# Moving the splits and sums behind the scan from GpSimd to VectorE in a one-core hybrid SSD / gated-MLP block

## The chip, the core and the metric

The kernel runs on one core of a Trainium2 chip, as one launch. The metric is the device time of one execution in microseconds. Five engines work side by side, each with a queue that it takes in order: TensorE (PE in the profile) for matmuls, ScalarE (ACT) for activations and copies, VectorE (DVE) and GpSimd (POOL) for elementwise work, SyncE (SP) for issuing DMAs. Matmul results land in PSUM; everything else is in SBUF or HBM.

## The reference, cut to what matters

```python
h   = rmsnorm(x, norm1_w) * (1 + sc1) + sh1          # sc1, sh1, g1, ... from c @ w_ada
proj = h @ w_in                                       # z, xbc, dt, sc_b, sc_c, sc_h
y_ssd = group_rmsnorm(ssd_scan(silu(conv(xbc)), dt) * silu(z))      # chunked scan
y_sc  = group_rmsnorm(sc_b * causal_dwconv(sc_c * sc_h, sc_conv_w)) # short convolution
x   = x + g1 * (concat(y_ssd, y_sc) @ w_out)          # out projection
h   = rmsnorm(x, norm2_w) * (1 + sc2) + sh2
u   = causal_dwconv(h @ w_up, ffn_conv_w) + ffn_conv_b # up projection, 2 x 2816 columns
x   = x + g2 * ((silu(u_gate) * u_value) @ w_down)    # down projection
out = rmsnorm(x)                                      # all float32, 1024 x 1024
```

## The kernel before, in words

**Number format.** Every large product is float32 made from three matmuls. `split` (lines 113 to 121) writes a rounded copy `hi` of a half page (128 x 512) with ScalarE (line 116) and the rest `lo = src - hi` with a second engine (line 117), VectorE unless `eng` names GpSimd; `mm3` (lines 123 to 127) then multiplies hi by hi, hi by lo and lo by hi. A matmul on an operand thus waits for one ScalarE and one VectorE or GpSimd instruction.

**Seven products instead of eight.** The short convolution, the out projection, the up and the down projection use a two-by-two scheme with seven block products (weights A11, A12, S1 to S4, A22; moving operands B11, B21, T1 to T4, B22). The weight sums S1 to S4 are made on the chip from the loaded halves: for a pair of weight pages `prep` (lines 539 to 571) issues two loads of 512 KB (lines 544, 545), four elementwise sums on the engine `sums` (line 558 for S3, line 561 for S2, S1 and S4, in place) and seven splits. The list that `prep` returns is emitted piecemeal between the products of the pair before (`take`).

**Stages, in order of time in the profiled execution.** Norm and first projection; the scan with the z projection (to about 380 us), in which GpSimd also sums weights for later (`combine`) and does two steps of the scan; the short convolution as 12 pairs (`prep_s(p)`, `pair_s`), whose sums are on VectorE for p = 0 to 3 and on GpSimd for p = 4 to 11; beside it `mod_half` (line 835) forms c @ w_ada on VectorE from loads of 256 KB; the out projection (about 600 to 776 us), where `product` calls `operand` for each step, which splits one half page of activations and one of weights, the weight's split on GpSimd in `m1` and `m2`; in `m2` GpSimd also subtracts two halves of y. Then the second norm (`x_norm`: ScalarE squares, eleven small VectorE instructions on 128 x 1, lines 97 to 106, a ScalarE scale), transposes, `half0` and `f1_tiles`, which make the moving operands B and T (`put` splits them; B22 and T4 and the difference behind T4 are on GpSimd); the up projection as 22 pairs (`prep_u(p)`), whose sums are on GpSimd except for p = 1; the down projection, which uses no GpSimd.

**What sets the order.** The engines' queues are not in the order of the text: a planner simulates the engines and emits, for each engine, the ready instruction that stands earliest; `tc.high_priority(offset=n)` lets instructions stand n places earlier. Which engine an instruction is on therefore also changes the order of the others on that engine. Buffers come from rings of fixed size: `raw` has 3 pages (4 in the up projection), `t3`, which holds the sum for S3, has one.

Of the kernel before, what the change touches and what calls it, by code (L numbers as in the profile page):

```python
# [36 lines left out]
def block_kernel(ctx: ExitStack, tc: tile.TileContext, x, crow, w_adat, w_m, w_z, w_dt,  # L37
                 w_out, w_up, w_down, vecs, rows, fnw, consts, out):
    nc = tc.nc
# [14 lines left out]
    def nm(s):  # L54
        uid[0] += 1
        return f"{s}{uid[0]}"

    def big():
        return pg.tile([P, T], F32, tag="pg", name=nm("pg"))

    def bank():
        return ps.tile([P, 512], F32, tag="ps", name=nm("ps"))
# [13 lines left out]
    def halves(page):  # L76
        return page[:, 0:512], page[:, 512:]
# [35 lines left out]
    def split(hi, lo, src, scale=None, eng=None):  # L113

        if scale is None:
            nc.scalar.activation(hi, src, AF.Copy)  # L116
            (eng or nc.vector).tensor_tensor(lo, src, hi.bitcast(F32), op=ALU.subtract)  # L117
        else:
            nc.scalar.activation(hi, src, AF.Copy, scale=scale)
            nc.vector.scalar_tensor_tensor(lo, src, scale, hi.bitcast(F32), op0=ALU.mult,  # L120
                                           op1=ALU.subtract)
# [125 lines left out]
    for k in range(ND):  # L247
# [3 lines left out]
        for q in range(2):  # L251
            s = slice(q * 512, q * 512 + 512)
            o = bank()
# [42 lines left out]
    o = bank()  # L296
# [34 lines left out]
    o = bank()  # L331
# [7 lines left out]
    o = bank()  # L339
# [46 lines left out]
    def sub(o, i0, i1, eng=None):  # L386
        (eng or nc.vector).tensor_tensor(o, i0, i1, op=ALU.subtract)  # L387
# [130 lines left out]
    wts = {}  # L518
# [20 lines left out]
    def prep(p, srcs, s3_tile, two, sums, early=None):  # L539

        rg, rv = wraw(), wraw()
        have = p in wts
        W = wts.setdefault(p, {})
        nc.sync.dma_start(rg, srcs[0])
        nc.sync.dma_start(rv, srcs[1])
        a11, a12 = halves(rg)
        a21, a22 = halves(rv)
        s3 = []

        def sp(name, src, eng=early):  # L550
            def f():
                W[name] = w_half()
                split(W[name][0], W[name][1], src if src is not None else s3[0], eng=eng)
            return f

        def sub3():
            s3.append(s3_tile())
            sums.tensor_tensor(s3[0], a11, a21, op=ALU.subtract)  # L558

        def tt(o, i0, i1, op):  # L560
            return lambda: sums.tensor_tensor(o, i0, i1, op=op)  # L561

        first = [] if have else [sp("A11", a11, None)] + ([sp("A12", a12, None)] if two else [])
        rest = [sub3, tt(a21, a21, a22, ALU.add), tt(a11, a21, a11, ALU.subtract),
                sp("S2", a11), sp("S1", a21), sp("S3", None)]
        if not two and not have:
            rest.append(sp("A12", a12))
        rest += [tt(a12, a12, a11, ALU.subtract), sp("S4", a12), sp("A22", a22)]
        if p == ("s", 0):
            rest.insert(7, rest.pop(5))  # L570
        return first + rest
# [6 lines left out]
    def prep_s(p):  # L578
        return prep(("s", p), [w_m[i] for i in spairs[p]],
                    lambda: psc[0].tile([P, 512], F32, tag="t3", bufs=1, name=nm("s3")), p < 2,  # L580
                    nc.gpsimd if p > 3 else nc.vector)

    psc = [None]

# [187 lines left out]
    with tc.high_priority(offset=100):  # L772
        for f in w0:
            f()
        gs, vl = big(), bank()
# [68 lines left out]
    for p in range(1, NS):  # L844
# [3 lines left out]
        gs, vl = (big(), nxt_vl) if p > 1 else (gs1, vl1)  # L848
# [114 lines left out]
    def acc_banks():  # L963
        return [bank() for c in range(4)]

    def big_banks():
        return [*halves(big()), *halves(big())]
# [11 lines left out]
    def dmm(o, c, op, start, stop, more=False):  # L979
        ah, al, bh, bl = op  # L980
        cs = slice(c * P, (c + 1) * P)
        mm3(o, ah[:, cs], al[:, cs], bh, bl, start, stop, more)
# [7 lines left out]
    def product(f, n, ring, o=None, i0=0, i1=None, pops=1, eng=None, more=False):  # L990

        o = o or acc_banks()
        for i in range(i0, n if i1 is None else i1):
            op = operand(f, i, ring, eng)
            for c in range(4):
                dmm(o[c], c, op, i == 0 and not more, i == n - 1, more)
            defer(pops)
        return o
# [13 lines left out]
    NM2 = 4  # L1012
# [18 lines left out]
    def load_o(i, page, half):  # L1031
        fetch()
        return ahead.pop(0)
# [4 lines left out]
    m1, _, _, _, m3, m7, m4 = sw_operands(Yo, load_o)  # L1038

    def m2(i):  # L1040
        gl, gr, vl, vr = Yo(i)
        return vl, load_o(i, 0, 1), [lambda: sub(gl, gl, gr, nc.gpsimd)]

    def m6(i):
        gl, gr, vl, vr = Yo(i)
# [54 lines left out]
    later += [lambda: ssd_load(1, (0, 1)), lambda: ssd_load(1, (2, 3)), last_pair]  # L1100
    later += [lambda: ssd_load(1, (4, 5)), lambda: ssd_load(1, (6, 7))]
    pgs = hhalf(F32)
    o = product(m1, 8, ring_o, i1=7, pops=2, eng=nc.gpsimd)
    later += [lambda i=i: sc_pair(i, 1) for i in range(3)]
    o2 = product(m2, 8, ring_o, big_banks(), i1=NM2, eng=nc.gpsimd)
    op = operand(m1, 7, ring_o)
    for c in range(4):
        dmm(o[c], c, op, False, True)
# [5 lines left out]
    for c in range(4):  # L1114
        nc.scalar.activation(acc[c], o[c], AF.Copy)
    oa = o
    o = product(m2, 8, ring_o, o2, NM2, eng=nc.gpsimd)
    c11 = hset()
    for c in range(4):
        add(c11[c], o[c], acc[c])  # L1120
# [50 lines left out]
    f0, f1 = [None] * ND, [None] * ND  # L1171

    def half0(k):
        f0[k] = f_tile(0, k)
        o = OPS["B11" if k < 4 else "B21"]
        o[k % 4] = hpage()
        split(o[k % 4][0], o[k % 4][1], f0[k], eng=nc.gpsimd if k % 2 else nc.vector)

    for c in range(4):
        later += [lambda c=c: gate(c12[c], c, 1), lambda c=c: x_norm(c)]  # L1180
# [17 lines left out]
    def prep_u(p):  # L1198
        def s3_tile():
            if p == 0:  # L1200
                return s3_first
            return pv[0].tile([P, 512], F32, tag="t3", bufs=1, name=nm("s3"))
        return prep(p, [w_up[2 * p], w_up[2 * p + 1]], s3_tile, p < 1,
                    nc.vector if p == 1 else nc.gpsimd, nc.gpsimd if p == 0 else None)

    w0 = prep_u(0)
    s3_first = yhalf()
# [4 lines left out]
    wts[1] = {}  # L1212
    for n, f in zip(("A11", "A12"), halves(t)):
        wts[1][n] = w_half()
        split(*wts[1][n], f, eng=nc.gpsimd)
    for f in w0[2:5]:
        f()
    w0 = w0[5:]
# [14 lines left out]
    def put(name, k, src, eng=None):  # L1233
        n = nput[0]
        nput[0] += 1
        if n < 8:
            d = hpage()
        elif n < 12:
            d = halves(tpage(F32R))
        elif n == 15:  # L1240
            d = small(F32R), small(F32R)
        else:
            d = yhalf(F32R), yhalf(F32R)
        OPS[name][k] = d
        split(d[0], d[1], src, eng=eng)
# [23 lines left out]
    w1 = prep_u(1)  # L1269
# [20 lines left out]
            put("T3", k, f1[k])  # L1290
        prod(V[0][0], "S3", "T3", 0, True, ks=[k])
    for k in range(4):
        put("B22", k, f1[k + 4], nc.gpsimd)
    for k in range(4):
        sub(f0[k + 4], f0[k + 4], f0[k], nc.gpsimd)
        put("T4", k, f0[k + 4], nc.gpsimd)
    hd = [pd.tile([P, T], F32, name=f"hd{p}") for p in range(NF - 1)]


# [66 lines left out]
    for p in range(NF):  # L1366
        nxt = w1 if p == 0 else prep_u(p + 1) if p + 1 < NF else sum(map(early_operand, range(3)), [])
        vl = V[p][0]
        if p > 1:
            G[p] = big()  # L1370
        gl, gr = halves(G[p])
# [34 lines left out]
    o = acc_banks()  # L1406
# [46 lines left out]
    m1, m2, m5, m6, m3, m7, m4 = sw_operands(Yd, load_d)  # L1453
# [17 lines left out]
    o = product(m1, NQ, ring, o, NE)  # L1471
# [4 lines left out]
    o = product(m2, NQ, ring)  # L1476
# [62 lines left out]
    o = product(m5, NQ, ring)  # L1539
# [3 lines left out]
    o = product(m6, NQ, ring)  # L1543
# [4 lines left out]
    o = product(m3, NQ, ring)  # L1548
# [4 lines left out]
    o = product(m7, NQ, ring)  # L1553
# [6 lines left out]
    o = product(m4, NQ, ring, [big()[:, 0:512], bank(), bank(), big()[:, 0:512]], i1=NQ - NL)  # L1560
# [87 lines left out]
```

## Time and profile before

| quantity | before |
|---|---|
| median of 3 runs | 1467.11 us (1466.14 to 1467.79) |
| profiled execution, its own time | 1469.52 us |
| span in that execution, first to last instruction | 1467.7 us |
| TensorE busy | 1388.9 us (95%), 6159 matmuls |
| VectorE busy | 1176.8 us (80%), 1882 instructions |
| ScalarE busy | 731.3 us (50%) |
| GpSimd busy | 309.3 us (21%), 213 instructions |
| mean granted TensorE clock | 0.979 of full speed |

Busy shares are means over stages with different limits, so the profile is read by stretches of the span. All times of rows are microseconds from the span's start unless marked ns. A matmul of 512 columns shows as some 0.39 us, but matmuls overlap, so TensorE is judged by its idle time and by the number of matmuls in a stretch. The granted clock stands at 1.00 (2.4 GHz) or 0.50 (1.2 GHz); a mean between them tells the share of the two in the stretch. Waiting instructions show as idle time in front of them, with the instruction that ended it.

### The profile page before, as it was taken

What the parts mean: (1) busy time and instruction counts of PE and PEld (TensorE: products, weight loads), DVE (VectorE), ACT (ScalarE), POOL (GpSimd) and SP (SyncE); (2) the same over time, 40 slices, a digit from 0 to 9 for tenths busy, and PEclk for the clock granted to TensorE, in tenths of its full rate; (3) what the DMA queues carried; (4) which work ended last, traced back from release to release, by engine and by line L of the source; (5) the groups of instructions that cost most, each with busy time, mean ns of one, the idle gap of its engine ahead of it and who ended that gap; (6) DMA issues with size and microseconds to landing.
All of it is one profiled execution on the core that took longest, in us unless ns stands there. A gap on an engine that the chain in (4) does not pass through costs nothing.

```text
span 1467.7 us, 17850 instructions
## 1 busy us (share of the span) xinstructions
PE 1388.9 (95%) x6159; PEld 1113.9 (76%) x6159; DVE 1176.8 (80%) x1882; ACT 731.3 (50%) x1272; POOL 309.3 (21%) x213
## 2 busy tenths in 40 slices
PE   4999999999999999998998699999999999999997
PEld 2788876777777777876886477888888888888885
DVE  7988868978898785599489799777777776889688
ACT  6633365666544434344486453444444444545463
POOL 0000032322012322261014733332333330000000
PEclk9999999999999999999999799999999999999999
DMA  8878964336454431785335132222222222856322
GB/s 319 299 267 316 310 199 164 136 103 222 152 173 154 140 122 61 253 253 184 114 116 172 58 129 101 86 86 82 77 87 86 87 86 101 316 207 209 100 101 101
DMA packets 89723, 232.18 MB, mean 158 GB/s; under 512 B 10296, under 2 KB 11016, under 8 KB 89632
## 3 DMA queue, kind: packets, MB, share of 16 engines
q1 hardware_dynamic: 89584, 231.00, 45.9%
q8 instruction: 48, 0.79, 0.2%
q14 instruction: 43, 0.35, 0.1%
q10 hardware_dynamic: 48, 0.05, 0.0%
HBM read 178.93 MB, written 52.08 MB: 157 GB/s over the span
## 4 chain that ended last, share of the span: by engine, by line
PE 63%; DVE 19%; DMA 6%; issue 5%; ACT 4%; POOL 1%; SPq 0%; DVEq 0%; POOLq 0%; ACTq 0%
PE ps L125 11%; PE ps L126 11%; PE ps L127 11%; PE pg L125 8%; PE pg L126 8%; PE pg L127 8%; DVE wl L117 3%; PE ps L485 2%; DVE sm L835 1%; DMA sm<-in_w_adat 1%; DMA cmb<-in_w_down 1%; ACT wh L116 1%; DVE cmb L387 1%; DVE T L373 1%; PE ps L493 1%
## 5 line engine op out<-in xcount | busy, mean ns | idle before, releaser
L116 ACT ACTIVATE wh<-raw 128x512 fp32r<-128x512 f32 (+1 forms) x272 | 173.0, 656 | 263.6 <-POOL raw L561 142.9
L117 DVE TENSOR_TENSOR wl<-raw,wh 128x512 fp32r<-128x512 f32 (+1 forms) x252 | 212.3, 855 | 78.7 <-ACT wh L116 72.6
L125 PE MATMUL pg<-H,wh 128*128 128x512 f32 x464 | 185.8, 402 | 10.5 <-ACT wh L116 6.2
L127 PE MATMUL pg<-H,wl 128*128 128x512 f32 x464 | 184.0, 397 | 1.7 <-DVE wl L117 1.7
L126 PE MATMUL pg<-H,wh 128*128 128x512 f32 x464 | 184.8, 398 | 0.4 <-DVE H L117 0.4
L125 PEld LDWEIGHTS pg<-H,wh 128*128 128x128 f32 x464 | 88.8, 192 | 32.1 <-ACT wh L116 7.3
L125 PE MATMUL ps<-H,wh 128*128 128x512 f32 x272 | 109.1, 402 | 3.8 <-ACT u L1265 3.8
L558 POOL TENSOR_TENSOR s<-raw,raw 128x512 f32<-128x512 f32 x28 | 53.5, 1912 | 278.4 <-DVE wl L117 166.6
L126 PE MATMUL ps<-H,wh 128*128 128x512 f32 x272 | 109.1, 401 | 3.2 <-DVE H L117 3.2
L127 PE MATMUL ps<-H,wl 128*128 128x512 f32 x272 | 108.0, 397 | 1.5 <-DVE wl L117 1.5
L126 PE MATMUL ps<-rg,rg 128*128 128x512 f32 x274 | 106.8, 390 | 0.0
L127 PE MATMUL ps<-rg,rg 128*128 128x512 f32 x274 | 106.6, 390 | 0.0
L127 PEld LDWEIGHTS pg<-H,wl 128*128 128x128 f32 x464 | 88.7, 191 | 21.5 <-DVE wl L117 3.2
L125 PE MATMUL ps<-rg 128*128 128x512 f32 x274 | 104.8, 390 | 0.0
L126 PEld LDWEIGHTS pg<-H,wh 128*128 128x128 f32 x464 | 88.7, 191 | 20.8 <-DVE H L117 2.5
L561 POOL TENSOR_TENSOR raw<-raw 128x512 f32<-128x512 f32 x58 | 85.9, 1492 | 78.6 <-DVE wl L117 69.1
L116 ACT ACTIVATE rg<-hp 128x512 fp32r<-128x512 f32 x85 | 51.6, 626 | 66.3 <-PE ps L127 46.1
L117 DVE TENSOR_TENSOR rg<-hp,rg 128x512 fp32r<-128x512 f32 x85 | 56.9, 684 | 18.2 <-ACT rg L116 18.0
L1330 DVE SCALAR_TENSOR_TENSOR cv<-ps,vec,cv 128x511 f32<-128x511 f32 (+2 forms) x132 | 67.8, 564 | 1.5 <-ACT cv L1326 1.4
L1309 DVE SCALAR_TENSOR_TENSOR cv<-pg,vec,cv 128x1023 f32<-128x1023 f32 (+1 forms) x44 | 56.2, 1277 | 15.4 <-ACT cv L1304 15.4
L662 DVE TENSOR_TENSOR pg<-pg,u 128x512 f32<-128x512 f32 x68 | 47.2, 694 | 25.3 <-PE pg L127 24.9
L487 POOL TENSOR_TENSOR xq<-xq,rw 128x512 f32<-128x512 f32 x16 | 19.0, 1186 | 221.3 <-issue 134.2
(379 smaller groups left out, 3513.5 us busy)
## 6 DMA issues: line engine op xcount, KB each, us to landing
raw<-in_w_up SPq DMA_DIRECT2D x45, 512.0 KB
raw<-in_w_m SPq DMA_DIRECT2D x36, 512.0 KB
sm<-in_w_adat SPq DMA_DIRECT2D x48, 256.0 KB
hd<-cv SPq DMA_DIRECT2D x21, 512.0 KB
hp<-hd SPq DMA_DIRECT2D x21, 512.0 KB
wr<-tdn SPq DMA_DIRECT2D x33, 256.0 KB
bc<-in_w_adat SPq DMA_DIRECT2D x16, 512.0 KB
seg<-ccd SPq DMA_DIRECT2D x16, 512.0 KB
```

The costliest lines, as they stand in the source:

```text
L116: nc.scalar.activation(hi, src, AF.Copy)
L117: (eng or nc.vector).tensor_tensor(lo, src, hi.bitcast(F32), op=ALU.subtract)
L125: nc.tensor.matmul(o, ah, bh, start=start, stop=False, skip_group_check=more)
L126: nc.tensor.matmul(o, ah, bl, start=False, stop=False, skip_group_check=more)
L127: nc.tensor.matmul(o, al, bh, start=False, stop=stop, skip_group_check=more)
L485: nc.tensor.matmul(y[:, h * HD:(h + 1) * HD], seg[:, h, :], xd[:, h * HD:(h + 1) * HD], start=True, stop=True)
L487: nc.gpsimd.tensor_tensor(hv(xg), hv(xg), rw[:, 2, g * 8:g * 8 + 8].unsqueeze(2).to_broadcast([P, 8, HD]), op=ALU.mult)
L558: sums.tensor_tensor(s3[0], a11, a21, op=ALU.subtract)
L561: return lambda: sums.tensor_tensor(o, i0, i1, op=op)
L662: nc.vector.tensor_tensor(o, i0, i1, op=ALU.add)
L1309: nc.vector.scalar_tensor_tensor(t[:, i:], g[:, :T - i], col(V_FW + (2 - i) * 44 + j), t[:, i:], op0=ALU.mult, op1=ALU.add)
L1330: nc.vector.scalar_tensor_tensor(o, v, col(V_FW + (2 - i) * 44 + j), o, op0=ALU.mult, op1=ALU.add)
```

## The change

All elementwise work that stood on GpSimd from the short convolution to the end of the up projection is given to VectorE: the four sums of `prep_s` for p = 4 to 11 (32 instructions), those of `prep_u` for p = 0 and p = 2 to 21 (84), the weight splits of `m1` and `m2` (15), the subtraction in `m2` (8), the odd splits of `half0` (4), the early splits of pair 0 and pair 1 of the up projection (7), the splits for B22 and T4 (8) and the subtraction for T4 (4): 162 instructions of 128 x 512 each. One piece of order changes as well: the first five entries of pair 1's list (three sums, the splits of S2 and S1) are emitted between the B22 splits and the T4 subtractions instead of later, in the loop. GpSimd keeps its work in the first projection and the scan. No DMA, matmul or ScalarE instruction is added or removed.

```diff
     def prep_s(p):
@@ in the call of prep
-                    nc.gpsimd if p > 3 else nc.vector)
+                    nc.vector)
     def m2(i):
         gl, gr, vl, vr = Yo(i)
-        return vl, load_o(i, 0, 1), [lambda: sub(gl, gl, gr, nc.gpsimd)]
+        return vl, load_o(i, 0, 1), [lambda: sub(gl, gl, gr)]
-    o = product(m1, 8, ring_o, i1=7, pops=2, eng=nc.gpsimd)
+    o = product(m1, 8, ring_o, i1=7, pops=2)
-    o2 = product(m2, 8, ring_o, big_banks(), i1=NM2, eng=nc.gpsimd)
+    o2 = product(m2, 8, ring_o, big_banks(), i1=NM2)
-    o = product(m2, 8, ring_o, o2, NM2, eng=nc.gpsimd)
+    o = product(m2, 8, ring_o, o2, NM2)
     def half0(k):
-        split(o[k % 4][0], o[k % 4][1], f0[k], eng=nc.gpsimd if k % 2 else nc.vector)
+        split(o[k % 4][0], o[k % 4][1], f0[k])
     def prep_u(p):
-                    nc.vector if p == 1 else nc.gpsimd, nc.gpsimd if p == 0 else None)
+                    nc.vector)
     for n, f in zip(("A11", "A12"), halves(t)):
-        split(*wts[1][n], f, eng=nc.gpsimd)
+        split(*wts[1][n], f)
     for k in range(4):
-        put("B22", k, f1[k + 4], nc.gpsimd)
+        put("B22", k, f1[k + 4])
+    for f in w1[:5]:
+        f()
+    w1 = w1[5:]
     for k in range(4):
-        sub(f0[k + 4], f0[k + 4], f0[k], nc.gpsimd)
-        put("T4", k, f0[k + 4], nc.gpsimd)
+        sub(f0[k + 4], f0[k + 4], f0[k])
+        put("T4", k, f0[k + 4])
```

## Rows read from the trace of the kernel before

**Rows 1.** Stretches: width; busy (instructions) of TensorE, weight loads, VectorE, ScalarE, GpSimd; clock; DMA

```profile
385.00:422.00 37.00, 36.68 (x159) 29.66 (x159) 34.73 (x65) 18.24 (x30) 0.00 (x0) 1.00 0.53 176
422.00:600.00 178.00, 170.61 (x719) 134.22 (x718) 132.77 (x214) 78.06 (x137) 45.93 (x32) 0.98 0.40 130
600.00:673.00 73.00, 66.98 (x291) 53.23 (x291) 59.15 (x73) 28.68 (x51) 36.97 (x23) 0.93 0.78 247
...
776.00:842.00 66.00, 49.58 (x193) 37.05 (x192) 54.73 (x95) 35.15 (x61) 41.49 (x26) 0.82 0.36 119
842.00:925.00 83.00, 76.76 (x325) 61.53 (x324) 74.32 (x110) 38.92 (x61) 28.11 (x17) 0.98 0.34 114
925.00:1225.00 300.00, 300.00 (x1315) 246.67 (x1314) 217.19 (x298) 139.17 (x219) 96.67 (x61) 1.00 0.24 85
```

**Rows 2.** TensorE's waits, whole span: total us, times, longest

```profile
PE ps L125 <- ACT u L1265: 6.2, 5, 3.1
PE pg L125 <- ACT wh L116: 6.2, 1, 6.2
PE ps L125 <- ACT u L733: 4.5, 2, 2.5
PE ps L1165 <- ACT xa L1156: 4.2, 1, 4.2
PE pg L126 <- POOL wl L117: 4.0, 3, 2.2
...
PE ps L126 <- DVE H L117: 3.2, 3, 1.9
...
PE pg L125 <- ACT u L733: 1.6, 2, 0.9
```

**Rows 3.** GpSimd's timeline, 551 to 557 us: start, duration

```profile
551.32 1.78 POOL L558 TENSOR_TENSOR s<-raw,raw 128x512 f32<-128x512 f32 x1 [5.92 <-DMA raw<-in_w_m]
553.18 1.61 POOL L561 TENSOR_TENSOR raw<-raw 128x512 f32<-128x512 f32 x1
554.87 1.26 POOL L561 TENSOR_TENSOR raw<-raw,raw 128x512 f32<-128x512 f32 x1
```

**Rows 4.** ScalarE's timeline, 556 us

```profile
556.16 0.63 ACT L116 ACTIVATE wh<-raw 128x512 fp32r<-128x512 f32 x1 [3.56 <-POOL raw L561]
556.70 0.58 ACT L733 ACTIVATE u<-ps 128x512 f32<-128x512 f32 x1
```

**Rows 5.** VectorE's timeline, 406 us

```profile
406.65 0.69 DVE L558 TENSOR_TENSOR s<-raw,raw 128x512 f32<-128x512 f32 x1
```

**Rows 6.** DMA issues on SyncE's queue, 403 us

```profile
403.02 0.33 SPq L545 DMA_DIRECT2D raw<-in_w_m  x1
```

**Rows 7.** Waits of all engines, 422 to 600 us: total us, times, longest

```profile
POOL s L558 <- DMA raw<-in_w_m: 111.8, 8, 70.0
```

**Rows 8.** VectorE's timeline where GpSimd is idle, 772 us, and 795 us

```profile
772.08 0.68 DVE L117 TENSOR_TENSOR wl<-ys,wh 128x512 fp32r<-128x512 f32 x1
772.69 0.68 DVE L117 TENSOR_TENSOR wl<-raw,wh 128x512 fp32r<-128x512 f32 x1
...
795.20 0.16 DVE L106 SCALAR_TENSOR_TENSOR rs<-rs,rs 128x1 f32<-128x1 f32 x1
```

**Rows 9.** VectorE's groups: 422:600, 600:673, 776:842, 842:925, one row each

```profile
L835 DVE SCALAR_TENSOR_TENSOR sm<-sm,cr 128x512 f32<-128x512 f32 x36 | 34.7, 974 | 8.9 <-DMA sm<-in_w_adat 8.9
...
L932 DVE SCALAR_TENSOR_TENSOR ys<-ys,vec,T 128x512 f32<-128x512 f32 x12 | 12.8, 1086 | 0.0
...
L106 DVE SCALAR_TENSOR_TENSOR rs<-rs,rs 128x1 f32<-128x1 f32 x12 | 6.1, 509 | 0.3
...
L163 DVE SCALAR_TENSOR_TENSOR ys<-ys,grow 128x512 f32<-128x512 f32 x14 | 14.5, 1049 | 5.5 <-DMA ys<-in_w_adat 5.4
```

**Rows 10.** GpSimd's timeline, 808 to 824 us

```profile
808.80 6.46 POOL L387 TENSOR_TENSOR ys<-ys,ys 128x512 f32<-128x512 f32 x1 [4.24 <-DVE ys L387]
...
822.39 1.72 POOL L387 TENSOR_TENSOR ys<-ys,ys 128x512 f32<-128x512 f32 x1
```

## The prediction

> **What bounds the kernel now.** I read the stretches first, then TensorE's waits, then the timelines around the longest of them. The page's 95% for TensorE says that little is to be had, but it is a mean. In 925 to 1225 us TensorE is busy 300.00 of 300 us with 1315 matmuls, 0.228 us each at the full clock [rows 1]: there nothing that VectorE or GpSimd does can be seen, and no gain is possible. The loss sits in four other stretches, where TensorE idles 7.4 us (422 to 600), 6.0 (600 to 673), 16.4 (776 to 842) and 6.2 (842 to 925), each the width less the busy time, 36 us in all [rows 1]. To this comes the clock: 0.82 in 776 to 842 means that some 36% of that stretch ran at 1.2 GHz; its 193 matmuls at 0.228 us are 44 us of work in 66, so idleness and clock cost 22 us there together [rows 1]. The reader is to see in the waits that most of the idle time is not put down to GpSimd by name: the copies `u` (L733, L1265) and a split `wh` on ScalarE are what TensorE waits for, GpSimd's own splits only 4.0 us [rows 2].
>
> The timelines show who stands behind these copies. At 551.32 us a load lands and GpSimd runs three dependent sums, 1.78, 1.61 and 1.26 us, to 556.13 [rows 3]. ScalarE, in order, holds the split of that sum at the head of its queue for 3.56 us, and the copy `u`, ready long before, goes only after it, at 556.70 [rows 4]; this is the 2.5 us of L733 [rows 2]. So GpSimd's slowness reaches TensorE by way of ScalarE's queue. In 385 to 422, the same loop with the sums on VectorE, TensorE idles 0.3 us in 37 [rows 1].
>
> **What GpSimd and VectorE cost each other.** With GpSimd idle, VectorE's splits of 128 x 512 take 0.68 us and start every 0.60 us, and a small `rs` step 0.16 us [rows 8]. Beside GpSimd, L835 means 974 ns, L932 1086, L163 1049, and the `rs` step L106 509 ns [rows 9]: instructions of either engine wait for the other. GpSimd suffers more: a subtraction took 1.72 us among VectorE's work, and one 6.46 us [rows 10].
>
> **The change, part by part.** 162 instructions go over at 0.60 us each, 97 us of new VectorE time. By stretch, from GpSimd's counts [rows 1]: 32 x 0.60 = 19.2; 23 x 0.60 = 13.8; 26 x 0.60 = 15.6; 17 x 0.60 = 10.2; 61 x 0.60 = 36.6. Against it VectorE gets back at least what the four rows show over 0.68 (0.16 for `rs`): 36 x 0.29 = 10.6; 12 x 0.41 = 4.9; 12 x 0.35 = 4.2; 14 x 0.37 = 5.2 [rows 9]. VectorE's load is then at most 132.8 + 19.2 - 10.6 = 141 of 178; 59.2 + 13.8 - 4.9 = 68 of 73; 54.7 + 15.6 - 4.2 = 66 of 66; 74.3 + 10.2 - 5.2 = 79 of 83; 217.2 + 36.6 = 254 of 300 [rows 1]. Work lands on the busier engine, yet its load hardly grows where the two collide; what goes is latency.
>
> - *Short convolution sums, 422 to 600.* Three sums take 1.8 us instead of 4.8, so ScalarE's copy is free 3.0 us sooner, more than any L733 wait (2.5). All of these, 4.5 + 1.6 = 6.1 us [rows 2], go; the clock of 0.98 stands for 0.02 x 178 = 3.6 us of lost work more, which may partly go with them [rows 1]. Bounds: a gain of 7.4 + 3.6 = 11, or a loss (first rival). New waits on VectorE's queue eat some. I take 6.
> - *Weight splits of the out projection, 600 to 673.* TensorE waited 4.0 us for GpSimd's `wl` [rows 2], which takes 0.68 us on VectorE. Bounds: all 6.0 us of idle time, or nothing, because VectorE is at 68 of 73 and each split stands in its queue. I take 4, the row's own value.
> - *Second norm and operands, 776 to 842.* The wait of 6.2 us for `wh` ends a chain that begins with the subtraction of 6.46 us [rows 2, 10]; on VectorE it is 0.68. With it goes part of the low clock that TensorE falls into after idling. The 4.2 us for `xa` [rows 2] hang on the `rs` steps, which lose 4.2 us to collisions [rows 9] but now share VectorE with seven early splits and four sums, 6.6 us: I count 1. The 3.2 us for `H` [rows 2] hang on VectorE's pace, and its load fills the stretch. Sum of the likely items 6.2 + 1 + 2 for the clock + 2 for `H` = 11; VectorE being full, I give back 3 and take 8. Bounds: 22 us (all lost time), or -2.4 (6.6 us of extra work less the 4.2 recovered, all of it ahead of `xa`).
> - *First pairs of the up projection, 842 to 925.* Load 74 to 79 of 83 at shorter latency; of 6.2 us idle I take 1. Bounds 6 and -5 (the load's growth). Pair 1's moved list issues no DMA; its three sums were on VectorE already, and its five entries now stand ahead of T4's eight instructions: nothing while `H` or `wh` is what comes last, 5 x 0.60 = 3.0 us if T4 is.
> - *Later pairs, 925 to 1225.* Zero: TensorE never waits, and VectorE keeps 46 us of slack. If that cover were gone, each pair's four sums would cost 2.4 us.
>
> SP's queue keeps its instructions. A load waits for its buffer's last split, so faster sums start loads no later.
>
> By its section "Optimizing Scalar/DVE Operations", the Trainium skill's page "Perfetto Trace Analysis" would rather move work off a saturated VectorE, even to GpSimd, and adds that a move between these two may not help as they share an SBUF read port. By that rule the three full stretches gain nothing, the second rival; here 36.97 us of GpSimd time in 600 to 673, which 13.8 us of VectorE replace [rows 1], speak against it in part.
>
> **Sum.** 6 + 4 + 8 + 1 = 19 us. The profiled execution took 1469.5 us, 1.8 more than its span; 1450.5 remain. It stood 2.4 us above the median of 1467.1, so the median to expect is 1448.
>
> **Rivals.**
> 1. *Slower: VectorE blocks on the loads.* GpSimd stood 41.8 us in seven waits, about 6 each, for `raw` to land (111.8 in 8, less the 70.0) [rows 7]. In VectorE's queue such a wait holds splits and additions too. A load takes 3.6 us from issue (403.02) to the sum that follows it (406.65) [rows 5, 6]. If the planner puts the first sum right behind the issue, eight pairs lose up to 3.6 each, 28.8, in place of the 7.4 now: 1467 + 21.4 - 13 for the other stretches = 1476. It decides from 2.6 us a pair on: (7.4 + 13) / 8. Against it: that sum at 406.65 shows no idle time before it [rows 5], and 385 to 422 runs without stalls [rows 1].
> 2. *VectorE is the bound.* From 600 to 925 its load is 93 to 100%; then the waits change name and only the short convolution's 6 us come: 1461.
> 3. *All of it.* Every wait behind GpSimd goes and the clock with it: of 36 idle us some 30, and 10 of the slow clock, less VectorE's own 3: 1467 - 37 = 1430. For it: how dense 385 to 422 is; against it: the loads above.
> That GpSimd stays in use behind the scan I rule out; the diff leaves no call there.
>
> **Chances.** Forecast 0.50, with a range of its own of 1440 to 1457; rival 1 0.17; rival 2 0.18; rival 3 0.15. This kernel's measurement tells about 0.2% (3 us) from no change. Faster: 0.50 + 0.15 + 0.11 of rival 2 = 0.76; same: 0.07 of rival 2 and 0.02 of rival 1 = 0.09; slower 0.15. The range 1434 to 1470 leaves out the lower half of rival 3 (0.08) and most of rival 1 (0.12).
>
> **What would show it.** GpSimd without an instruction after the scan; L835 and L163 near 0.69 us; L733's waits of TensorE near nothing; no wait of 6 us at about 815, and a clock of 0.9 or more in that stretch; 925 to 1225 unchanged. Wrong would be VectorE waiting for `raw<-in_w_m` in front of L558 (rival 1), or TensorE waiting as long as before for VectorE's `wl` and `H` (rival 2).

## The result and the profile after

| quantity | after |
|---|---|
| median, 4 runs | 1424.1 us (1421.47 to 1424.72) |
| before beside it, 4 runs | 1466.62 us (1464.99 to 1467.79) |
| ratio | 0.9707, 95% interval 0.9691 to 0.9724 |
| span of the profiled execution | 1422.4 us, clock 0.988 |

The change made the kernel 42.5 us faster. The forecast was 19 us, 1448, and its range ended at 1434; the direction was right, the size was not. The third rival (all of it, 1430) came nearest.

First the page of after, its engines' busy time:

```profile
span 1422.4 us, 17691 instructions
## 1 busy us (share of the span) xinstructions
PE 1374.3 (97%) x6159; PEld 1106.7 (78%) x6159; DVE 1187.6 (83%) x2044; ACT 733.9 (52%) x1272; POOL 53.9 (4%) x51
```

VectorE runs 162 instructions more than before and is busy only 10.8 us longer (1176.8 before). At the pitch of 0.60 us [rows 8] the 162 are 97 us; so the 1882 instructions that it had already became some 86 us cheaper (an estimate from these numbers). GpSimd's last instruction stands in the scan:

```profile
350.84 1.96 POOL L487 TENSOR_TENSOR xq<-xq,rw 128x512 f32<-128x512 f32 x1 [10.13 <-DVE xd L482]
```

Next the stretches of after, cut so that each holds the matmuls of one of [rows 1] (or of two neighbours), with the same columns:

```profile
385.00:422.00 37.00, 36.69 (x159) 29.62 (x159) 34.55 (x65) 18.24 (x30) 0.00 (x0) 1.00 0.53 176
422.00:587.00 165.00, 165.00 (x719) 132.33 (x718) 131.72 (x247) 78.41 (x137) 0.00 (x0) 1.00 0.44 141
587.00:650.00 63.00, 62.50 (x291) 51.97 (x292) 51.30 (x88) 28.18 (x49) 0.00 (x0) 0.97 0.85 273
650.00:753.00 103.00, 102.90 (x468) 84.46 (x467) 85.48 (x174) 65.96 (x126) 0.00 (x0) 1.00 0.40 139
753.00:802.00 49.00, 43.42 (x175) 31.64 (x174) 43.89 (x106) 33.34 (x59) 0.00 (x0) 0.90 0.34 118
802.00:880.00 78.00, 78.00 (x343) 64.19 (x343) 74.03 (x121) 41.34 (x64) 0.00 (x0) 1.00 0.38 125
880.00:1180.00 300.00, 300.00 (x1315) 246.37 (x1315) 243.16 (x380) 141.26 (x218) 0.00 (x0) 1.00 0.26 91
```

Read by matmuls: the 719 of the short convolution took 178 us and take 165; the next 291 took 73 and take 63; the 518 of the second norm and the first pairs of the up projection took 66 + 83 = 149 and take 49 + 78 = 127; the 1315 after them took 300 and take 300. The gains of 13 + 10 + 22 = 45 us are the whole difference of the two profiled spans (1467.7 - 1422.4 = 45.3); the profiled execution of before stood 2.9 us above its median of 1466.62, so the medians differ by less, 42.5. In the short convolution TensorE is now busy all of its time at the full clock.

TensorE's waits of after, to set against [rows 2]:

```profile
PE ps L255 <- DVE X L223: 16.1, 2, 15.8
PE pg L125 <- ACT H L116: 3.0, 2, 2.7
PE ps L125 <- ACT H L116: 2.3, 2, 1.1
PE ps L126 <- DVE H L117: 0.9, 1, 0.9
...
PE pg L125 <- ACT p L1265: 0.7, 1, 0.7
PE ps L125 <- ACT u L1265: 0.5, 1, 0.5
```

The first is in the prologue and stood there before. The 6.2 us for `wh`, everything behind the copy `u` of L733, the 4.0 us for GpSimd's `wl` and the 4.2 us for `xa` are gone; the copy `u` of L1265 fell from 6.2 to 0.5. VectorE has one new wait of some size, for the loads in front of the first sum of a pair:

```profile
DVE s L558 <- DMA raw<-in_w_m: 10.1, 6, 2.4
```

And VectorE's groups of after:

```profile
L117 DVE TENSOR_TENSOR wl<-raw,wh 128x512 fp32r<-128x512 f32 x252 | 168.9, 684 | 22.9 <-ACT wh L116 20.9 <-PE ps L702 0.9
L835 DVE SCALAR_TENSOR_TENSOR sm<-sm,cr 128x512 f32<-128x512 f32 x48 | 32.2, 685 | 3.9 <-DMA sm<-in_w_adat 3.8
L163 DVE SCALAR_TENSOR_TENSOR ys<-ys,grow 128x512 f32<-128x512 f32 x16 | 10.6, 686 | 3.7 <-DMA ys<-in_w_adat 3.7
```

In the kernel before the first of these was

```profile
L117 DVE TENSOR_TENSOR wl<-raw,wh 128x512 fp32r<-128x512 f32 x232 | 188.0, 824 | 77.4 <-ACT wh L116 71.4 <-PE ps L702 5.3
```

Twenty splits more cost 19 us less: beside GpSimd each of the 232 had taken 0.14 us more. This group, the largest on VectorE, has no row in the prediction's sum.

### The profile page after: what moved, and what is told of

Its sections match the earlier page's. It is cut to its first block, busy times and chain, and to the rows that moved or that the text cites. A ratio compares the mean times of both kernels' runs of the same rounds, so it can differ in the third digit from the quotient of the medians.

```text
span 1422.4 us, 17691 instructions
## 1 busy us (share of the span) xinstructions
PE 1374.3 (97%) x6159; PEld 1106.7 (78%) x6159; DVE 1187.6 (83%) x2044; ACT 733.9 (52%) x1272; POOL 53.9 (4%) x51
## 4 chain that ended last, share of the span: by engine, by line
PE 76%; DVE 12%; DMA 6%; issue 2%; ACT 2%; SPq 1%; POOL 0%; DVEq 0%; ACTq 0%; POOLq 0%
PE ps L125 14%; PE ps L126 14%; PE ps L127 14%; PE pg L126 10%; PE pg L125 9%; PE pg L127 9%; PE ps L485 2%; DVE wl L117 1%; DVE T L373 1%; DVE cmb L387 1%; DMA cmb<-in_w_down 1%; PE ps L493 1%; DMA tout<-cmb 1%; DMA cmb<-in_w_out 1%; PE ps L501 1%
## 5 line engine op out<-in xcount | busy, mean ns | idle before, releaser
L117 DVE TENSOR_TENSOR wl<-raw,wh 128x512 fp32r<-128x512 f32 (+1 forms) x272 | 193.2, 723 | 23.6 <-ACT wh L116 21.5
L125 PE MATMUL ps<-H,wh 128*128 128x512 f32 x272 | 107.9, 397 | 2.8 <-ACT H L116 2.3
L126 PE MATMUL ps<-H,wh 128*128 128x512 f32 x272 | 107.3, 394 | 0.9 <-DVE H L117 0.9
L125 PEld LDWEIGHTS ps<-H,wh 128*128 128x128 f32 x272 | 51.3, 189 | 15.9 <-ACT H L116 3.1
L126 PEld LDWEIGHTS ps<-H,wh 128*128 128x128 f32 x272 | 51.3, 189 | 12.9 <-DVE H L117 1.6
L127 PEld LDWEIGHTS ps<-H,wl 128*128 128x128 f32 x272 | 51.4, 189 | 11.4 <-DVE wl L117 0.3
```

Source lines behind the costliest of these rows:

```text
L125: nc.tensor.matmul(o, ah, bh, start=start, stop=False, skip_group_check=more)
L126: nc.tensor.matmul(o, ah, bl, start=False, stop=False, skip_group_check=more)
L127: nc.tensor.matmul(o, al, bh, start=False, stop=stop, skip_group_check=more)
```

## The experiments

Three theories stood against each other. **P, VectorE's pace:** GpSimd's instructions slow VectorE's own, by collision, and VectorE is late for TensorE. **Q, the queue** (L in the last two runs; the prediction's own path): GpSimd's results come late, hold ScalarE's queue, and lateness is what TensorE sees. **O, the order:** the planner emits other queues once an engine changes, and that is the gain. Times are medians, each with its ratio to the kernel before, which was run beside it on the same chip. The kernel before took 1463.2 to 1467.2 us from one chip to another, so runs of different rows are compared by their ratios.

To see where a kernel gains I use landmarks: first and last starts of lines that occur once. They are of before. Columns: count, shortest/median/longest ns, first to last start, shape.

```profile
L702 PE MATMUL ps<-sq,sel x12: 397/399/424, 436.2 to 580.2; 128*32 128x512 f32 x12
L1068 PE MATMUL pg<-cst,H x32: 165/252/355, 616.5 to 620.1; 128*128 128x2 f32 x32
L1165 PE MATMUL pg<-cst,xa x32: 271/273/330, 751.8 to 763.7; 128*128 128x128 f32 x32
L1165 PE MATMUL ps<-cst,xa x32: 270/273/477, 791.2 to 803.3; 128*128 128x128 f32 x32
L179 PE MATMUL ps<-cst,g x2: 271/272/273, 464.1 to 1211.3; 128*8 128x128 f32 x2
```

The same of after:

```profile
L702 PE MATMUL ps<-sq,sel x12: 392/398/400, 435.0 to 567.2; 128*32 128x512 f32 x12
L1068 PE MATMUL pg<-cst,H x32: 165/251/251, 603.4 to 606.8; 128*128 128x2 f32 x32
L1165 PE MATMUL pg<-cst,xa x32: 270/272/329, 728.8 to 740.6; 128*128 128x128 f32 x32
L1165 PE MATMUL ps<-cst,xa x32: 270/273/330, 768.1 to 777.0; 128*128 128x128 f32 x32
L179 PE MATMUL ps<-cst,g x2: 271/272/272, 461.5 to 1166.0; 128*8 128x128 f32 x2
```

So the short convolution (L702's first to L1068's first) took 180.3 and takes 168.4 us. The table has this and three more intervals for every run: "out", L1068's first to L1165's first; "middle", from there to L1165's last; "up", from there to L179's last. Each row is one profiled execution. "Up" reads 405.0 to 408.0 in the four rows whose edit touches nothing there (before, p1_sc, p2_out, m1_kept) and "short conv." 180.3 to 182.3 in its four (before, p2_out, p3_mid, p4_up), so differences of 2 or 3 us in these columns say nothing.

| run | us | ratio, 95% interval | short conv. | out | middle | up |
|---|---|---|---|---|---|---|
| before | 1466.62 | 1 | 180.3 | 135.3 | 51.5 | 408.0 |
| after | 1424.10 | 0.9707 (0.9691 to 0.9724) | 168.4 | 125.4 | 48.2 | 389.0 |
| p1_sc | 1452.06 | 0.9923 (0.9899 to 0.9948) | 168.2 | 135.4 | 52.8 | 405.2 |
| p2_out | 1454.99 | 0.9934 (0.9914 to 0.9955) | 181.1 | 127.0 | 52.3 | 405.9 |
| p3_mid | 1453.11 | 0.9921 (0.9900 to 0.9942) | 180.3 | 135.4 | 48.1 | 397.4 |
| p4_up | 1455.02 | 0.9934 (0.9916 to 0.9951) | 182.3 | 134.6 | 52.3 | 395.0 |
| o1_nomove | 1420.34 | 0.9693 (0.9667 to 0.9718) | 168.4 | 127.0 | 48.2 | 388.8 |
| d1_sc_up | 1452.46 | 0.9913 (0.9891 to 0.9934) | 191.1 | 126.9 | 49.1 | 395.8 |
| d2_out_mid | 1458.60 | 0.9962 (0.9945 to 0.9978) | 172.1 | 142.0 | 62.5 | 395.3 |
| d3_memset | 1420.79 | 0.9696 (0.9662 to 0.9731) | 168.3 | 125.3 | 48.8 | 388.7 |
| q1_late | 1419.73 | 0.9689 (0.9651 to 0.9727) | 170.1 | 125.3 | 48.3 | 388.0 |
| m1_kept | 1464.09 | 1.0005 (0.9987 to 1.0022) | 177.2 | 134.6 | 52.5 | 405.0 |
| k2_fill | 1443.76 | 0.9845 (0.9830 to 0.9859) | 170.7 | 134.6 | 49.6 | 401.1 |
| k3_fill | 1446.44 | 0.9862 (0.9845 to 0.9878) | 171.1 | 134.8 | 51.0 | 396.1 |
| s1_scan | 1438.73 | 0.9816 (0.9793 to 0.9839) | 168.4 | 127.0 | 48.6 | 388.0 |
| s2_comb | 1420.08 | 0.9697 (0.9669 to 0.9726) | 168.7 | 123.7 | 48.2 | 389.5 |

**One part of the change at a time**, on the kernel before. Only the sums of the short convolution:

```diff
     def prep_s(p):
-                    nc.gpsimd if p > 3 else nc.vector)
+                    nc.vector)
```

> The kernel before with only the short convolution's sums (32 instructions) on VectorE. Theory Q (queues: TensorE lost time because ScalarE and the matmuls behind it waited for GpSimd's slow chains; each part pays in its own stretch): 13 us faster than before, some 1454, the 719 matmuls of 422 to 600 us in 165 us instead of 178, all later stretches as before. Theory O (order: most of the gain is the planner's new order of the queues, for which all parts are needed): under 6 us, or shifts in stretches that the part does not touch. As the prediction had it: 6 us.

Only the splits of `m1` and `m2` and the subtraction of `m2`:

```diff
-    o = product(m1, 8, ring_o, i1=7, pops=2, eng=nc.gpsimd)
+    o = product(m1, 8, ring_o, i1=7, pops=2)
...
-        return vl, load_o(i, 0, 1), [lambda: sub(gl, gl, gr, nc.gpsimd)]
+        return vl, load_o(i, 0, 1), [lambda: sub(gl, gl, gr)]
```

> The kernel before with only the out projection's 15 weight splits and 8 subtractions on VectorE. Theory Q: 10 us faster, some 1457, the 291 matmuls after the short convolution in 63 instead of 73 us, nothing elsewhere. Theory O: under 4 us, or gains elsewhere. As the prediction had it: 4 us.

Only `half0`, pairs 0 and 1 of the up projection, B22, T4 and the moved list:

```diff
     def prep_u(p):
-                    nc.vector if p == 1 else nc.gpsimd, nc.gpsimd if p == 0 else None)
+                    nc.vector if p < 2 else nc.gpsimd)
...
-        put("B22", k, f1[k + 4], nc.gpsimd)
+        put("B22", k, f1[k + 4])
```

> The kernel before with only the work between the out projection and the pairs of the up projection on VectorE (odd splits of half0, early splits and sums of pair 0, splits of pair 1, B22, T4 and the moved list): 27 instructions. Theory Q: the stretch from 776 us on loses 12 to 15 us, some 1453; the first pairs (842 to 925) stay as they were, because their sums stay on GpSimd. Theory O: under 6 us. As the prediction had it: 8 us.

Only the sums of pairs 2 to 21:

```diff
     def prep_u(p):
-                    nc.vector if p == 1 else nc.gpsimd, nc.gpsimd if p == 0 else None)
+                    nc.gpsimd if p == 0 else nc.vector, nc.gpsimd if p == 0 else None)
```

> The kernel before with only the sums of pairs 2 to 21 of the up projection (80 instructions) on VectorE. Theory Q: 7 us faster, some 1460, all of it in 842 to 925 us; 925 to 1225 stays at 300 us for 1315 matmuls. Theory O: about nothing alone. As the prediction had it: 1 us.

Measured: gains of 0.77, 0.66, 0.79 and 0.66%, together 2.88% against 2.93% for the whole change. Each part pays in its own interval and elsewhere by no more than such rows differ anyway: p1_sc takes 12.1 us from the short convolution, p2_out 8.3 from "out", p3_mid 3.4 from "middle" and 10.6 from "up", p4_up 13.0 from "up". O had expected under 6 us, under 4, under 6 and about nothing; and in the trace of p1_sc all 6159 matmuls stand in the order of before. So O falls here. P and Q both fit: they differ in the two kinds of run that follow.

**The moved list undone**, on the kernel after:

```diff
-    for f in w1[:5]:
-        f()
-    w1 = w1[5:]
```

> The changed kernel without its one change of order: pair 1's list is emitted in the loop again. Theory Q: the same within 3 us, since only five entries stand elsewhere. Theory O: 5 us or more slower, in 753 to 802 us.

Measured: not to be told from after. The piece of order that the change moves by hand is worth nothing that this run can tell.

**GpSimd collides, but nobody waits for it.** On the kernel after, GpSimd gets sums again whose results are not used. `dead` adds a loaded half page to a scratch of constants that has no other use any more; four per pair where the change took four away:

```diff
+    def dead(a, n=1, d=cst[:, C_CC:C_CC + 512]):
+        [nc.gpsimd.tensor_tensor(d, a, d, op=ALU.add) for _ in range(n)]
...
-            sums.tensor_tensor(s3[0], a11, a21, op=ALU.subtract)
+            sums.tensor_tensor(s3[0], a11, a21, op=ALU.subtract)
+            dead(a22, 4)                     # pairs 4 to 11 and 2 to 21
```

> The changed kernel with a dead load on GpSimd: as many sums as before (four for each pair 4 to 11 of the short convolution and 2 to 21 of the up projection) on a tile that nobody reads, started by the same loads; the queues of the four other engines are in the same order as in the changed kernel. Nobody waits for GpSimd, but its instructions collide with VectorE's. Theory Q (the slow chains in the queues were the loss): within 3 us of the changed kernel, 1424; the 719 matmuls of the short convolution stay at 165 to 167 us, the first pairs at 78 to 80 us, although L835 goes back to 0.9 us or more. Theory P (port: VectorE stretched by collisions was the loss): half of 13 + 9 us or more comes back, 1435 and more. No output of the reference is changed.

The same for the out projection and the middle, one dead sum per moved instruction:

```diff
-        split(h[:, 512:], l[:, 512:], w, eng=eng)
+        split(h[:, 512:], l[:, 512:], w); dead(w)
...
-        put("B22", k, f1[k + 4])
+        put("B22", k, f1[k + 4]); dead(f1[k + 4])
```

> The changed kernel with a dead load on GpSimd of the same kind in the other two places: one dead sum for each split or sum that was moved in the out projection and between it and the pairs of the up projection (50 in all). Theory Q: within 3 us of the changed kernel. Theory P: half of 10 + 13 us or more comes back, 1435 and more, because VectorE is 97% busy there.

Measured: Q's expectation fell. By the ratios d1_sc_up lost 2.06% of the gain of 2.93%, some 30 us, and d2_out_mid 2.55%, some 37. In both traces all matmuls stand in the order of after, and nothing waits for the dead sums but SyncE's queue, once, for 1.1 us (d2_out_mid). The page of d1_sc_up and two of its groups:

```profile
PE 1380.3 (95%) x6159; PEld 1106.7 (76%) x6159; DVE 1242.7 (86%) x2044; ACT 733.7 (51%) x1272; POOL 226.0 (16%) x163
```

```profile
L572 POOL TENSOR_TENSOR cst<-raw,cst 128x512 f32<-128x512 f32 x112 | 171.1, 1527 | 660.0 <-DMA raw<-in_w_up 471.2 <-DMA raw<-in_w_m 182.2
...
L117 DVE TENSOR_TENSOR wl<-raw,wh 128x512 fp32r<-128x512 f32 x252 | 196.2, 792 | 20.1 <-ACT wh L116 19.2
...
L835 DVE SCALAR_TENSOR_TENSOR sm<-sm,cr 128x512 f32<-128x512 f32 x48 | 36.4, 774 | 1.9 <-DMA sm<-in_w_adat 1.9
```

VectorE's same 2044 instructions take 55 us longer (1242.7 against 1187.6); splits go from 684 to 792 ns. And TensorE's waits in 420 to 625 us of this kernel:

```profile
PE ps L125 <- ACT u L733: 7.9, 2, 5.9
PE ps L702 <- DVE sq L117: 5.2, 4, 3.3
PE pg L125 <- ACT u L733: 2.8, 2, 1.4
```

The very name on which the prediction built its path, the copy `u` of L733, is back, with no sum of GpSimd in front of any ScalarE instruction. A wait's name is who came last, not what made it late. The short convolution, 191.1 us, is even slower than before: there VectorE now carries the sums as well, and its in-place sums (L561) lengthen too, from 684 to 810 ns.

**GpSimd as busy, without reading.** Memsets of the scratch in place of the dead sums, 8 per pair behind one sum of 8 columns:

```diff
+    def dead(a, d=cst[:, C_CC:C_CC + 512]):
+        nc.gpsimd.tensor_tensor(d[:, 0:8], a[:, 0:8], d[:, 0:8], op=ALU.add)
+        [nc.gpsimd.memset(d, 1.0) for _ in range(8)]
```

> The changed kernel with a dead load on GpSimd in the same places as the dead sums (pairs 4 to 11 of the short convolution, 2 to 21 of the up projection), started by the same loads, but eight memsets of 128x512 per pair, which read nothing from SBUF, behind one small sum of 128x8 that starts them. The queues of the other engines are unchanged. Theory P1 (VectorE and GpSimd contend for reads): the changed kernel's time within 4 us, 1424, the short convolution's 719 matmuls in 165 us, L835 at 0.69 us. Theory P2 (any busy GpSimd slows VectorE, or holds something else up): 10 us or more slower, as with the dead sums, and L835 at 0.9 us or more.

Measured: 1420.79, as after. The page and two groups:

```profile
PE 1370.3 (97%) x6159; PEld 1103.5 (78%) x6159; DVE 1188.4 (84%) x2044; ACT 734.4 (52%) x1272; POOL 184.2 (13%) x303
```

```profile
L572 POOL MEMSET cst<- 128x512 f32 x224 | 118.2, 528 | 12.9
...
L835 DVE SCALAR_TENSOR_TENSOR sm<-sm,cr 128x512 f32<-128x512 f32 x48 | 32.1, 685 | 3.7 <-DMA sm<-in_w_adat 3.2 <-DVE sm L835 0.4
```

118 us of writing by GpSimd add 0.8 us to VectorE's busy time; 171 us of adding, which reads and writes, added 55. What collides here is GpSimd's reading. The Trainium skill's page "SBUF — State Buffer", section "Who interferes with whom", says the same: a VectorE instruction with two inputs in SBUF contends with a GpSimd instruction that reads SBUF, not with one that only writes it. The traces agree: 774 and 685 ns in L835.

**Lateness without collisions.** On the kernel after, ScalarE's split of S2 in pairs 4 to 11 has to wait for eight memsets on GpSimd, 8 x 0.526 = 4.2 us, that begin when its sum is there:

```diff
+    def late(hi, lo, a, d=cst[:, C_CC:C_CC + 512]):
+        nc.gpsimd.tensor_tensor(d[:, 0:8], a[:, 0:8], d[:, 0:8], op=ALU.add)
+        [nc.gpsimd.memset(d, 1.0) for _ in range(8)]
+        nc.scalar.activation(hi, a, AF.Copy, scale=d[:, 0:1])
+        nc.vector.tensor_tensor(lo, a, hi.bitcast(F32), op=ALU.subtract)
```

> The changed kernel with lateness alone in the short convolution: for pairs 4 to 11 ScalarE's split of S2 also waits for eight memsets on GpSimd, which begin when the sum S2 is there and read nothing from SBUF; the value that the last one writes is a scale of one. Lateness as with GpSimd's chain of sums or more, without its collisions. Theory Q (late splits at the head of ScalarE's queue): 422 to 587 us gets 6 to 13 us longer, some 1433. Theory P (collisions): within 3 us of the changed kernel, since the planner lets other instructions go first.

Measured: 1419.73, and 1.7 us in its own interval (170.1 against 168.4). ScalarE did stand still for GpSimd, in all eight pairs:

```profile
ACT wh L572 <- POOL cst L572: 18.6, 8, 4.1
```

TensorE's waits in 415 to 585 us of this kernel are 1.0 us in all. On the kernel after, where the sums themselves come early, a queue that is held so costs next to nothing.

**The blocked queue removed**, on the kernel before: the copies `u`, `u2`, `u3` leave ScalarE's queue for VectorE.

```diff
-        nc.scalar.activation(t, src, AF.Copy)          # L733
+        nc.vector.tensor_copy(t, src)
```

> The kernel before with the copies u, u2, u3 of the short convolution (L733) on VectorE instead of ScalarE, the sums still on GpSimd. Theory Q: the waits of TensorE for L733 (6.1 us) go, since the copies stand no more behind a split that waits for GpSimd; 5 to 10 us faster in 422 to 600 us, some 1459. Theory P: no gain, or slower by up to 10 us, as 36 more instructions of 0.6 us on VectorE collide with GpSimd's sums.

Measured: ratio 1.0005, no gain; in the short convolution 3.1 of the 11.9 us. TensorE's waits there, 420 to 605 us:

```profile
PE ps L125 <- DVE u L733: 2.7, 4, 1.1
PE ps L125 <- ACT sq L695: 2.0, 2, 1.4
PE pg L125 <- DVE u L733: 1.8, 3, 1.3
PE ps L702 <- DVE sq L117: 0.5, 2, 0.3
```

7.0 us in all against 7.4 of idle time before: the wait changed its name. Alone, this run does not decide: the copies also give VectorE 36 more instructions in a stretch where it shares time with GpSimd (148.0 us busy in 420 to 600, 132.8 before in 422 to 600), which may have eaten a gain. That the head of ScalarE's queue was a symptom is shown by the next two runs.

**The kernel before with the reading alone removed.** The runs so far stand on the kernel after, with a fuller VectorE. The last two show the size at before's own working point: GpSimd keeps every sum of the pairs as a step, with its waits, but adds only 8 of the 512 columns and writes the half page by memsets.

```diff
+        def summ(o, a, b, op):               # where sums is nc.gpsimd
+            nc.gpsimd.tensor_tensor(o[:, 0:8], a[:, 0:8], b[:, 0:8], op=op)
+            [nc.gpsimd.memset(o, 1.0) for _ in range(2)]      # k3_fill: 3
...
-            sums.tensor_tensor(s3[0], a11, a21, op=ALU.subtract)
+            summ(s3[0], a11, a21, ALU.subtract)
```

> Left out: of the kernel before's sums on GpSimd in the weight pairs (short convolution pairs 4 to 11, up projection pairs 0 and 2 to 21) only the first 8 of 512 columns are computed; two memsets of the whole half page follow in place of the rest. They read nothing, stay on GpSimd, take the operands' landing and the buffers' order as before, and last as long as the sums did: 0.36 + 2 x 0.53 = 1.42 us against 45.93 / 32 = 1.44 in 422 to 600. So GpSimd is as late as before, and only the reading of 128 x 512 operands beside VectorE is gone. If collisions made the loss (theory P): the two parts that moved these sums gained 13.7 and 10.7 us, so some 24 us, 1443; from L702's first start to L1068's 168 us instead of 180.3, from the last of L1165 to L179 some 395 instead of 408. If lateness made it (theory L, the prediction's own: the chain of slow sums holds ScalarE's queue): as before, 1464 to 1469, with 180 and 408.

> Left out as with two memsets, but with three, so that each of these steps on GpSimd takes 0.36 + 3 x 0.53 = 1.94 us, later than the sums of the kernel before (1.44 in 422 to 600, 1.58 in 925 to 1225). Theory P: still faster than before by most of 24 us, 1443 to 1450, within 5 us of the run with two memsets. Theory L: slower than before, by some 0.5 us x 3 sums for each of 8 pairs of the short convolution, 1475 to 1480, with 190 us from L702's first start to L1068's.

Measured: 1443.76, where P said 1443 and L 1464 to 1469; and 1446.44 with three memsets, intervals that overlap. The short convolution takes 170.7 and 171.1 us, where P said 168 and L 180 (with three memsets 190). "Up" takes 401.1 and 396.1; for k2_fill P said 395 and L 408, and it fell between the two. The page of k2_fill, then its groups:

```profile
PE 1377.8 (95%) x6159; PEld 1106.5 (77%) x6159; DVE 1125.9 (78%) x1882; ACT 734.5 (51%) x1272; POOL 296.4 (21%) x445
```

```profile
L117 DVE TENSOR_TENSOR wl<-raw,wh 128x512 fp32r<-128x512 f32 x232 | 160.4, 703 | 59.7 <-ACT wh L116 52.9 <-PE ps L702 6.1
...
L540 POOL MEMSET raw<- 128x512 f32 x174 | 91.5, 526 | 8.4
L835 DVE SCALAR_TENSOR_TENSOR sm<-sm,cr 128x512 f32<-128x512 f32 x48 | 32.3, 687 | 13.9 <-DMA sm<-in_w_adat 13.7
L540 POOL MEMSET s<- 128x512 f32 x56 | 29.5, 526 | 1.7
L540 POOL TENSOR_TENSOR s<-raw,raw 128x8 f32<-128x8 f32 x28 | 24.5, 874 | 274.9 <-DVE wl L117 166.9 <-DMA raw<-in_w_m 108.0
```

GpSimd is as busy as before (296 of 309 us), and a step for S3 lasts 0.87 + 2 x 0.53 = 1.93 us, as the whole sum did in the kernel before:

```profile
L558 POOL TENSOR_TENSOR s<-raw,raw 128x512 f32<-128x512 f32 x28 | 53.5, 1912 | 278.4 <-DVE wl L117 166.6 <-DMA raw<-in_w_m 111.8
```

Was the lateness kept? In the short convolution it was. ScalarE's wait for GpSimd's sums, in 422 to 600 us of before and in the same work of k2_fill (418 to 586):

```profile
ACT wh L116 <- POOL raw L561: 33.8, 12, 6.5
...
ACT wh L116 <- POOL raw L540: 29.8, 13, 4.9
```

With three memsets it is 31.6 us (415 to 584). TensorE's waits for `u` of L733 were 4.5 + 1.6 = 6.1 us before [rows 2]; k2_fill has one row of them, and this stretch, with the columns of [rows 1]:

```profile
PE ps L125 <- ACT u L733: 1.9, 2, 1.5
```

```profile
418.00:586.00 168.00, 166.13 (x722) 132.92 (x721) 112.53 (x215) 79.20 (x138) 41.30 (x96) 1.00 0.43 140
```

So ScalarE's queue is held as long as before and TensorE no longer feels it; what fell is VectorE's busy time for the same work, from 132.8 [rows 1] to 112.5 us. In the up projection lateness was kept less well: from L1165 on, ScalarE's wait for GpSimd's sums is 109.1 us before, 48.2 in k2_fill and 68.4 with three memsets.

VectorE's 1882 instructions, the same as before, are 51 us cheaper in all (1125.9 against 1176.8), and the kernel is 1.55% faster, as much as p1_sc and p4_up together (0.77 + 0.66 = 1.43%) within the intervals. TensorE's order is not the reason: 6155 of its 6159 matmuls stand in k2_fill's trace in the order of before. The gain of moving these sums is thus collisions that end: shown in the short convolution up to some 2.5 us (170.7 against p1_sc's 168.2), and the likely reading in the up projection.

**How far it carries.** GpSimd still works in the scan. On the kernel after, first all of it that remains in the scan (L487, L506 and the weight sums of `combine`, L391) on VectorE, then only `combine`:

```diff
-        eng = nc.gpsimd if pages else None   # L391, both runs
+        eng = None
...
-        nc.gpsimd.tensor_tensor(hv(xg), hv(xg),             # L487, s1_scan alone
+        nc.vector.tensor_tensor(hv(xg), hv(xg),
...
-                nc.gpsimd.tensor_tensor(hv(ns), hv(state[g]), hc(Cd), op=ALU.mult)   # L506, s1_scan
+                nc.vector.tensor_tensor(hv(ns), hv(state[g]), hc(Cd), op=ALU.mult)
```

> The changed kernel with GpSimd's work in the scan on VectorE as well (L487, L506 and the sums of combine, 38 instructions). If slow chains are what costs, 2 to 5 us faster in 190 to 385 us, some 1420; if VectorE, 17 of 20 us busy there, becomes the bound, 5 to 10 us slower, some 1432.

> The changed kernel with only the sums of combine in the scan (10 instructions) on VectorE as well, L487 and L506 still on GpSimd. All the scan's work on VectorE had made it 12 us slower there. If it was the ten sums that hurt, 5 to 10 us slower than the changed kernel, some 1431; if it was L487 and L506, which stand in the chain from one chunk's state to the next, within 3 us or up to 4 us faster, some 1421.

Measured: s1_scan is 1438.73, worse than after; s2_comb, 1420.08, cannot be told from it. The landmark of s1_scan shows where it loses:

```profile
L702 PE MATMUL ps<-sq,sel x12: 391/398/401, 446.7 to 579.0; 128*32 128x512 f32 x12
```

L702 begins at 446.7 us, where it begins at 427.6 to 435.0 in after and in all other runs on it, and the rest is as after. So the move does not pay everywhere: these steps are worth more on GpSimd, in spite of collisions. VectorE's busy time from 190 us to L702 grew by only 5.6 us for 33 instructions more (208.3 to 213.9), so it is not simply full; ScalarE's wait for VectorE's L638 there grew from 17.2 to 38.2 us. Which of L487 and L506 carries the loss, and by what path, was not tried. No version clearly beats the kernel after: o1_nomove, d3_memset, q1_late and s2_comb lie within its interval of ratios or overlap it.

## Why the prediction was wrong

- **The step that failed** is the one that says "So GpSimd's slowness reaches TensorE by way of ScalarE's queue" and, after it, "what goes is latency". The rows of [rows 3, 4] are true, but they show the last link. What made TensorE late in the short convolution was VectorE's pace. k2_fill kept ScalarE's wait for GpSimd there (29.8 us for 33.8) and took 9.6 us from the short convolution and 1.55%, 22.7 us, from the kernel; k3_fill's longer steps did much the same; q1_late added lateness for 1.7 us; m1_kept freed the queue for nothing.
- **The term that was mis-sized** is what VectorE gets back. The sum counted 10.6 + 4.9 + 4.2 + 5.2 = 25 us "at least", from four groups [rows 9], and went on as if that were the amount. Measured are some 86 us of 97. The largest group, 232 splits at 824 ns, was left out, and with it the other sums, subtractions and small steps that run on VectorE beside GpSimd. Over all groups of VectorE, count times the loss of the mean against after adds up to 84 us. The forecast loads of 141, 68 and 145 us in the three stretches (the last two of the second norm and the first pairs added) stand against 131.7, 51.3 and 117.9 measured.
- **Short convolution, 6 us forecast, 13 measured.** The bound of 11 was passed. Idle time and clock made 11.0; by matmuls, 719 x 0.228 = 164 us of work stood in 178, so 14 were lost. Some three of them show neither as a gap nor as a low clock in the rows.
- **Out projection, 4 forecast, 10 measured.** I priced only the wait that names GpSimd. The bound of 6.0 was passed, as it left out the clock of 0.93, another 0.07 x 73 = 5 us. Pricing all 291 matmuls at 0.228 us would not do here, since 48 of them are narrow (32 of 2 columns, 16 of 128). The landmarks give 9.9 for the whole of "out", p2_out alone 9.7 (0.66%).
- **776 to 925, 8 + 1 forecast, 22 measured.** The first pairs are the larger miss: p4_up alone gains 9.7 us (0.66%), nearly all of it there, against 1; p3_mid 11.6 (0.79%) against 8. The likely items summed to 11 in the first part, and I gave 3 back for "VectorE being full". VectorE was full of collisions: the rows show 227 instructions where there were 205, and 117.9 us busy where it was 129.05. (The forecast counted 43 more in these stretches; the planner placed the others in the rows beside them.) The clock rose with it, 0.90 and 1.00 for 0.82 and 0.98. The "44 us of work in 66" also counted 32 matmuls of 128 columns (L1165) as wide ones, so more than 22 us were lost there.
- **Later pairs, 0 forecast, 0 measured**: 300 us for 1315 matmuls in both, with VectorE up from 217 to 243. Right, and for the reason given: TensorE never waited there.
- **The rivals.** VectorE blocked on loads (first rival; its sum gives 1475, not 1476): its sign came, but small, 10.1 us in six waits in front of L558, 1.7 us each and 2.4 at the longest, under the 2.6 us a pair from which it would decide. The short convolution is dense all the same. VectorE the bound (second): refuted, in 802 to 880 us TensorE is busy 78.00 of 78 with VectorE at 74.0. The third, "of 36 idle us some 30, and 10 of the slow clock, less VectorE's own 3", came nearest in size, but by adding up waits and clock; it, too, had no term for VectorE's pace.
- **The signs named in advance** came: no GpSimd instruction behind the scan, L835 and L163 at 0.685 and 0.686 us, no wait on L733, 925 to 1225 unchanged. The clock of 0.9 came as well. They told that the change worked as an edit; they fit lateness and collisions alike, and say nothing of the size.

Open is how the 42.5 us divide between collisions and lateness in the out projection and the middle, where no run kept the one and removed the other: d2_out_mid shows that dead sums cost some 37 us there on the fuller VectorE, more than the 21 us (0.66 + 0.79%) that p2_out and p3_mid gain, so collisions suffice, but lateness is not excluded. In the out projection there is a path of it that the prediction did not name: in 590 to 780 us of before, SyncE's queue stands 15.9 us in five waits (9.0 the longest) for GpSimd's `wl` splits to give a load (L1028) its buffer, and in p2_out these waits are gone.

## What to carry to other kernels

Where VectorE and GpSimd overlap, price a move by what VectorE's own instructions lose beside GpSimd (mean of every two-input group against its mean with GpSimd idle, times the count), before pricing latency; here a move of 97 us onto an engine at 80% raised its busy time by 11. In the scan the same move lost time (s1_scan), so try each stretch by itself. Size the loss of a stretch by the count of its full-width matmuls times the pace of a dense stretch, not by the idle time alone, and take the name of a wait as the last link only. To tell collision from lateness, replace the suspected reads by writes of the same length.

## What the runs showed of the hardware

- Dead sums on GpSimd, on a kernel that waits for none of them, cost VectorE 55 us for 171 us of GpSimd time (d1_sc_up), and memsets of 118 us cost it 0.8 (d3_memset). A memset of 128 x 512 took 0.525 to 0.537 us in all 224 cases of d3_memset, beside a VectorE that is busy 84% of the time, while the sums of before took 1.36 to 1.91 us by group.
- GpSimd loses as well, and not in proportion to its work: sums of 8 columns took 0.24 and 0.27 us in two groups of k2_fill and 0.87 us in the one shown above, where single ones took 0.20 to 2.32 us.
